# Prompt attention scores by three rounded products of high and low parts, and new sample value rows sent by GpSimd's queue, in a two-layer hybrid encoder step

## The chip, the cores and the metric

The kernel runs on one core of one Trainium2 chip. The metric is device time in microseconds of one execution. All times below are from runs and one profiled execution of the kernel before the change, with the TensorE clock granted in full (1.000) throughout.

## What is computed

The reference is one inference step of a two-layer encoder. 512 prompt frames and 8 x 16 sample frames, 640 columns in all, share the weights; the model width is 1024, the feed-forward width 2816. Per layer:

```
x += 1/2 * SwiGLU_1(RMSNorm(x))
z  = RMSNorm(x) @ w_in              # conv B | conv C | conv V | q | k | v | gates
conv branch: y_c = B * causal_depthwise_conv3(C * V)
attn branch: 8 heads x 64; prompt frames attend to the prompt up to their own 64-frame chunk,
             sample frames to 256 cached rows and their own 16
             s = (q @ k.T) * 64 ** -0.5 + rel_bias[distance];  softmax;  @ v
x += (sigmoid(g_c) * (y_c @ w_conv_out) + sigmoid(g_a) * (y_a @ w_attn_out)) @ w_o
x += 1/2 * SwiGLU_2(RMSNorm(x))
```

A final RMSNorm follows. The new keys, values and conv states are outputs too. Everything is float32.

## The kernel before

**Layout and arithmetic.** Features lie on the 128 partitions and the 640 columns (`T`) along the free dimension, in two halves of 320 (`HT`). Nearly all products with weights are computed from rounded parts: a float32 tile is split into a high part, which ScalarE rounds into an `fp32r` tile (`ACT.copy`), and a low part, which VectorE takes as the difference (`DVE.tensor_tensor`, subtract; `split`, `prep` and `flush`, L364 and L369). A product is then the sum of three TensorE matmuls, high x high, high x low and low x high (`multiply` L431, `block` L453; the matmul's line in the trace is L435 or L459). Weights come through SyncE's DMA queue in slabs (`raw`), are split into `whi` and `wlo` a slab or two ahead, and pairs of output tiles are formed by a scheme of seven products for eight (`seven`, L833), which runs as a generator: each `yield` lies behind six matmuls of 320 columns.

**The mixer of a layer.** `attention` (L1782) runs while the projections of `w_in` are computed. `qk(p)` (L1796) forms queries and keys of head pair p (two heads of 64 features, on partitions 0 to 63 and 64 to 127). In `both`, called by it, the last steps are: the second half of k (columns 320 to 639) is scaled behind the fifth product (`lo2`), q is completed behind the sixth (`up2`, then `queries`, which multiplies by `rr`, the reciprocal of the RMS, and by 64 ** -0.5, L1802), and the first half of k behind the seventh (`lo1`, L1368). `keys` sends k to the output by GpSimd's queue and copies the sample's columns.

**Prompt scores.** `scores(p)` (L1859) multiplies q by k for both heads of a pair, causal block rows i = 3, then 1, then 0 and 2, with (i + 1) * 128 key columns each. The two heads stand on the two halves of the partitions, so the contraction has 64 rows. Before the change q and k are plain float32 tiles, with two buffers each:

```
for i, c in spans:
    for e in range(2):
        r = slice(e * HD, (e + 1) * HD)
        PE.matmul(pss[e][:, c], qa[p][r, i * P : (i + 1) * P], ka[p][r, : (i + 1) * P],
                  start=True, stop=True)
```

The trace holds two records for each float32 matmul, so the 8 matmuls of one call of `scores` are 16 records (L1882). VectorE then adds the bias and takes the row maximum out of PSUM (L1888; `CUSTOM_DVE_ANT_0` in the trace, `ISA` in the instruction order), ScalarE does the softmax (L2082, L1899), TensorE transposes (L1919) and multiplies by v (L1951).

**What sets the order.** TensorE's order in this stage is the order of the code: calls of `scores`, `turn` and `values` with `fill(n)` between them, which runs n steps of the stream of projections (qk(1), qk(2), qk(3), then conv and gates). `scores(0)` comes two steps behind the end of qk(0); `scores(1)` and `scores(2)` three steps behind the end of their own qk; `scores(3)` three steps behind qk(3), and directly behind `values(1)`. The orders of VectorE, ScalarE, GpSimd and SyncE in this stage are made by the scheduler, by priorities (`soon` raises them).

**Samples.** For each of the 8 samples, `sscores` (L1986) loads cached keys into tiles of the tags "q" and "k" (the buffers that the prompt's q and k use) and cached values, clears a tile `vn` on GpSimd and copies the sample's 16 new value rows into it by a DMA from SyncE's queue (L2000). `svalues` (L2032) multiplies by them later (L2040).

Of the kernel before, what the change touches and what calls it, by code (L numbers as in the profile page):

```python
# [196 lines left out]
def trunk(ctx: ExitStack, tc: tile.TileContext, xin, wst, small, pbias, samplebias, kcache, vcache, gfin,  # L197
# [33 lines left out]
    def tmp(name):  # L231
        return tp.tile([P, UW], F32, tag="t", name=name)[:, :T]
# [191 lines left out]
    def soon():  # L424
        return tc.high_priority(offset=300)
# [908 lines left out]
    def mixer(l, after):  # L1334
        with tc.tile_pool(name=f"yp{l}", bufs=1, reuse_waits="tile") as yp, \
# [18 lines left out]
            with tc.tile_pool(name=f"mp{l}", bufs=2, reuse_waits="tile") as mp:  # L1354
# [3 lines left out]
                def pair(n, *given):  # L1358
                    return seven(f"{l}_{n}", pr, ops.X, *cs, *given)

                def upper(u):

                    return lambda pb: add(u[:, t1], pb, cs[0]), lambda pc: add(u[:, t2], pc, cs[1])

                def lower(g, scale=-1.0):

                    def by(c, src):
                        DVE.scalar_tensor_tensor(out=g[:, c], in0=src, scalar=scale, in1=rr[:, c],  # L1368
                                                 op0=ALU.mult, op1=ALU.mult)

                    def second(pa):
                        add(g[:, t2], pa, cs[2])
                        by(t2, g[:, t2])

                    return second, lambda pa: by(t1, pa)

                def both(n, u, g, third, last, scale=-1.0):

                    (up1, up2), (lo2, lo1) = upper(u), lower(g, scale)

                    def end1(pc):
                        up2(pc)
                        third()

                    def end2(pa):
                        lo1(pa)
                        last()

                    return pair(n, up1, lo2, end1, end2)

                def gate_pair(m):
                    u, g = gates[m], gates[m + 1] = tmp(f"g{l}_{m}"), tmp(f"g{l}_{m + 1}")
# [52 lines left out]
    class Operands:  # L1445
# [24 lines left out]
        def parts(self, hi, lo, z):  # L1470
            ACT.copy(hi, z)
            DVE.tensor_tensor(out=lo, in0=z, in1=hi.bitcast(F32), op=ALU.subtract)
# [309 lines left out]
    def attention(l, h, norms, stats, ops, mp, yas, ycp, both, others):  # L1782
# [12 lines left out]

        def qk(p):  # L1796

            q = qa[p] = mp.tile([P, T], F32, name=f"q{l}_{p}", tag="q")
            k = ka[p] = mp.tile([P, T], F32, name=f"k{l}_{p}", tag="k")

            def queries():
                DVE.scalar_tensor_tensor(out=q, in0=q, scalar=HD ** -0.5, in1=rr, op0=ALU.mult, op1=ALU.mult)  # L1802
                for e in range(2):
                    r = slice(e * HD, (e + 1) * HD)
                    POOL.tensor_copy(bd[r, :, p, e * TS : (e + 1) * TS],
                                     q[r, SEQ:].rearrange("p (b t) -> p b t", b=NB))

            def keys():
                POOL.dma_start(ko[l, :, p, :], k)
                POOL.tensor_copy(ks[:, p, :], k[:, SEQ:])  # L1810

            return both(f"qk{p}", q, k, queries, keys)

        def work():
            for p in range(1, npair):
# [43 lines left out]
        def scores(p):  # L1859

            heads = [2 * p + e for e in range(2)]
            bias, ss, st = [], [], []
            for hh in heads:
                n = f"{l}_{hh}"
                bias.append(mp.tile([P, SEQ], F32, name=f"bias{n}", tag="bias"))
                POOL.dma_start(bias[-1], pbias[l, hh])
                POOL.memset(bias[-1][0:CHUNK, SEQ - CHUNK :], NEG)

                ss.append(mp.tile([P, offs[-1] + SEQ], F32, name=f"s{n}", tag="s") if p % 2
                          else ycp[hh % 2].rearrange("p a t -> p (a t)"))  # L1870
                st.append(mp.tile([P, 2, NQ], F32, name=f"st{n}", tag="st", bufs=4))

            for rows in ((3,), (1,), (0, 2)):
                pss = [(pr if rows == (1,) else att)(f"pss{l}_{hh}_{rows[0]}") for hh in heads]
                spans, o = [], 0
                for i in rows:
                    spans.append((i, slice(o, o + (i + 1) * P)))
                    o = spans[-1][1].stop
                for i, c in spans:
                    for e in range(2):  # L1880
                        r = slice(e * HD, (e + 1) * HD)
                        PE.matmul(pss[e][:, c], qa[p][r, i * P : (i + 1) * P], ka[p][r, : (i + 1) * P],  # L1882
                                  start=True, stop=True)
                for i, c in spans:
                    for e in range(2):
                        w = (i + 1) * P
                        with soon():
                            DVE.tensor_tensor_reduce(  # L1888
                                out=ss[e][:, offs[i] : offs[i] + w], in0=pss[e][:, c],
                                in1=bias[e][:, SEQ - w :], scale=1.0, scalar=NEG, op0=ALU.add,  # L1890
                                op1=ALU.max, accum_out=st[e][:, 0, i : i + 1])
            for e, hh in enumerate(heads):
                weigh(hh, ss[e], st[e])
# [92 lines left out]
        def sscores(b):  # L1986
# [10 lines left out]

            vn = mp.tile([P, SEQ], F32, name=f"vn{n}", tag="bias")[:, :AW]
            POOL.memset(vn, 0.0)
            SP.dma_start(vn[:TS], vnew[rows])  # L2000
            for e, kc in enumerate(kcs):
                POOL.tensor_copy(kc[:, :, PAST:], ks[:, e * npair // 2 : (e + 1) * npair // 2, rows])
            pss = att(f"spss{n}")[:, :KS]
# [432 lines left out]
```

## Time and profile before

| | |
|---|---|
| median of 3 runs | 2481.9 us (2481.69 to 2482.22) |
| the profiled execution's own time | 2481.95 us |
| its span, first to last instruction | 2480.2 us |
| TensorE / VectorE / ScalarE / GpSimd busy | 99% / 88% / 56% / 13% of the span |
| prompt scores: 8 calls (4 head pairs, 2 layers) | 16 records each, 2.36 us each |
| the longest single wait of TensorE for another engine | 5.3 us, at the start of the program |

Busy time is the time in which an engine has an instruction under way. Matmuls overlap, and their recorded durations include the way through the array, so the pace of TensorE is read from the starts of successive matmuls, not from the mean duration of one. In the profile L followed by a number is the line in the kernel; PE is TensorE, PEld its weight loads, DVE VectorE, ACT ScalarE, POOL GpSimd, SP SyncE; a small q behind an engine's name is its queue. `pss` is the PSUM tile of the scores.

### The profile page before, as it was taken

Reading aid. Unit: us, or ns where it says so; the run is one execution under the profiler, and the core shown is the slowest. Engines: PE = TensorE matmul, PEld = TensorE weight load, DVE = VectorE, ACT = ScalarE, POOL = GpSimd, SP = SyncE. Lnnn points to the kernel's source line nnn. Section 1 sums busy time; section 2 is a strip of 40 time slices with the busy share of each in tenths; the row PEclk is TensorE's granted clock in tenths of the full one; section 3 lists DMA queues with packets and bytes.
Section 4 is the critical chain, followed back from the end, with each engine's and each line's share of the span. In section 5 each row is a group of like instructions: output and inputs, shape, how many; then the busy total and the mean of one; then the engine's idle time right before and its main releaser. Section 6 shows DMA issues by size and latency. Waiting matters only on the chain.

```text
span 2480.2 us, 44054 instructions
## 1 busy us (share of the span) xinstructions
PE 2467.0 (99%) x17264; PEld 2414.6 (97%) x17264; DVE 2182.4 (88%) x3643; ACT 1385.6 (56%) x2230; POOL 319.5 (13%) x483
## 2 busy tenths in 40 slices
PE   9999999999999999999999999999999999999999
PEld 8999999889999999999999999998899999999998
DVE  7999998888888899998799999988888889999997
ACT  6555556675555555555665555566655556555555
POOL 0111112211000001111001010121110000111111
PEclk9999999999999999999999999999999999999999
DMA  4443444335344334444334343452453333444444
GB/s 155 127 117 102 120 118 125 110 114 174 99 118 124 94 102 107 112 118 118 110 94 109 110 117 102 117 128 103 137 167 94 118 119 93 107 113 107 112 117 117
DMA packets 113520, 288.16 MB, mean 116 GB/s; under 512 B 12992, under 2 KB 52544, under 8 KB 113312
## 3 DMA queue, kind: packets, MB, share of 16 engines
q1 hardware_dynamic: 69552, 220.10, 27.0%
q0 software_dynamic: 43328, 64.99, 13.8%
q8 instruction: 135, 2.21, 0.4%
q14 instruction: 73, 0.60, 0.1%
q10 hardware_dynamic: 432, 0.25, 0.0%
HBM read 239.48 MB, written 7.94 MB: 100 GB/s over the span
## 4 chain that ended last, share of the span: by engine, by line
PE 93%; DVE 3%; ACT 2%; issue 1%; DMA 1%; SPq 0%; DVEq 0%; ACTq 0%; POOLq 0%
PE pab L459 12%; PE paa L459 11%; PE pcb L459 6%; PE daa L1144 6%; PE pca L459 5%; PE dab L1144 5%; PE po L435 5%; PE qa L459 4%; PE pbb L459 3%; PE dca L1144 3%; PE pba L459 3%; PE dcb L1144 2%; PE ma_cv L459 2%; PE ma_qk L459 2%; PE py L435 2%; PE pv L1835 2%
## 5 line engine op out<-in xcount | busy, mean ns | idle before, releaser
L364 ACT CAST whi<-raw 128x512 fp32r<-128x512 f32 (+1 forms) x577 | 501.7, 874 | 371.6 <-PE pbb L459 46.0
L369 DVE TENSOR_TENSOR wlo<-raw,whi 128x512 fp32r<-128x512 f32 (+1 forms) x577 | 577.1, 1002 | 137.1 <-ACT whi L364 132.9
L364 ACT CAST whi<-s 128x1024 fp32r<-128x1024 f32 (+1 forms) x162 | 152.8, 943 | 320.3 <-DVE s L296 113.9
L459 PE MATMUL pab<-xhib,whi 128*128 128x320 f32 x704 | 217.7, 309 | 0.0
L459 PE MATMUL pab<-xlob,whi 128*128 128x320 f32 x704 | 217.3, 309 | 0.0
L459 PE MATMUL pab<-xhib,wlo 128*128 128x320 f32 x704 | 217.3, 309 | 0.0
L459 PE MATMUL paa<-xhia,whi 128*128 128x320 f32 x640 | 197.8, 309 | 0.2 <-DVE ga L296 0.2
L459 PE MATMUL paa<-xhia,wlo 128*128 128x320 f32 x640 | 197.6, 309 | 0.0
L459 PE MATMUL paa<-xloa,whi 128*128 128x320 f32 x640 | 197.5, 309 | 0.0
L369 DVE TENSOR_TENSOR wlo<-s,whi 128x1024 fp32r<-128x1024 f32 (+1 forms) x162 | 176.4, 1089 | 4.4 <-ACT whi L364 4.4
L1166 POOL DMA_DIRECT2D x<-c_a x80 | 69.8, 1019 | 575.2 <-ACT ahia L1048 205.5
L1166 POOL DMA_DIRECT2D x<-c_b x72 | 63.1, 1011 | 583.2 <-ACT ahib L1048 205.4
L459 PEld LDWEIGHTS pab<-xhib,whi 128*128 128x128 f32 x704 | 132.1, 188 | 0.9 <-issue 0.9
L459 PEld LDWEIGHTS pab<-xlob,whi 128*128 128x128 f32 x704 | 132.1, 188 | 0.0
L459 PEld LDWEIGHTS pab<-xhib,wlo 128*128 128x128 f32 x704 | 132.1, 188 | 0.0
L459 PEld LDWEIGHTS paa<-xhia,whi 128*128 128x128 f32 x640 | 120.1, 188 | 1.1 <-DVE ga L296 0.5
L459 PEld LDWEIGHTS paa<-xloa,whi 128*128 128x128 f32 x640 | 120.1, 188 | 0.3 <-DVE xloa L703 0.3
L459 PEld LDWEIGHTS paa<-xhia,wlo 128*128 128x128 f32 x640 | 120.1, 188 | 0.2
L296 DVE TENSOR_TENSOR raw<-s,raw 128x512 f32<-128x512 f32 x162 | 110.8, 684 | 0.0
L459 PE MATMUL pcb<-xhib,wlo 128*128 128x320 f32 x352 | 108.9, 309 | 0.0
L459 PE MATMUL pcb<-xlob,whi 128*128 128x320 f32 x352 | 108.7, 309 | 0.0
L459 PE MATMUL pcb<-xhib,whi 128*128 128x320 f32 x352 | 108.7, 309 | 0.0
(909 smaller groups left out, 8200.5 us busy)
## 6 DMA issues: line engine op xcount, KB each, us to landing
raw<-in_wst SPq DMA_DIRECT2D x375, 512.0 KB, 3.6
x<-c_a POOLq DMA_DIRECT2D x80, 160.0 KB, 4.9
x<-c_b POOLq DMA_DIRECT2D x72, 160.0 KB, 4.2
lent<-in_wst POOLq DMA_DIRECT2D x36, 256.0 KB, 3.7
kc<-in_kcache SPq DMA_DIRECT2D x32, 256.0 KB, 4.9
vc<-in_vcache SPq DMA_DIRECT2D x16, 512.0 KB, 4.3
one<-in_wst POOLq DMA_DIRECT2D x32, 256.0 KB, 3.9
x<-u_a POOLq DMA_DIRECT2D x40, 160.0 KB, 4.1
```

What stands on the lines that cost most here:

```text
L296: DVE.tensor_tensor(out=out, in0=a, in1=b, op=op)
L364: ACT.copy(hi[:, d], src[:, c])
L369: DVE.tensor_tensor(out=lo, in0=src, in1=hi.bitcast(F32), op=ALU.subtract)
L435: PE.matmul(ps[:, a, :HT], w, x[a] if isinstance(x, tuple) else x[:, a * HT : (a + 1) * HT], start=first and j == 0 and not seeded, stop=l ...
L459: PE.matmul(ps, a, b, start=start and kp == 0 and j == 0, stop=stop and kp == NP - 1 and j == 2, skip_group_check=True)
L1144: PE.matmul(ps[u], w, y, start=start and i == 0 and j == 0, stop=i == 1 and j == 2, skip_group_check=True)
L1166: POOL.dma_start(x[ms[2 * u + r]][:, cols], z[:, u], accum_op=ALU.add)
L1835: PE.matmul(pv[t], xx[:, t * P : (t + 1) * P], w[:, kk * AW : (kk + 1) * AW], start=c == 0 and kk == 0 and j == 0, stop=c == KT // 2 - 1 a ...
```

## The change

1. `qk(p)` now puts q and k into temporary tiles (the pool of four that the gates and the conv use) and makes from each a pair of `fp32r` tiles of 512 columns, high and low. Each pair takes both buffers of its tag. `parts` does it: a rounding copy on ScalarE and a subtraction on VectorE. q is split in one piece of 512 columns after it is complete, k in two: columns 320 to 511 in the middle of `both` (the new argument `mid`), columns 0 to 319 behind its last product.
2. `scores(p)` computes each block as three matmuls into the same PSUM region: q high x k high, q low x k high, q high x k low, for both heads in turn, each on its 64 partitions. Its place in TensorE's stream is as it was.
3. The copy of a sample's new value rows into `vn` is issued from GpSimd's queue instead of SyncE's.

```diff
@@ -1374,9 +1374,14 @@
 
                     return second, lambda pa: by(t1, pa)
 
-                def both(n, u, g, third, last, scale=-1.0):
+                def both(n, u, g, third, last, scale=-1.0, mid=None):
 
                     (up1, up2), (lo2, lo1) = upper(u), lower(g, scale)
+
+                    def half(pa):
+                        lo2(pa)
+                        if mid:
+                            mid()
 
                     def end1(pc):
                         up2(pc)
@@ -1386,7 +1391,7 @@
                         lo1(pa)
                         last()
 
-                    return pair(n, up1, lo2, end1, end2)
+                    return pair(n, up1, half, end1, end2)
 
                 def gate_pair(m):
                     u, g = gates[m], gates[m + 1] = tmp(f"g{l}_{m}"), tmp(f"g{l}_{m + 1}")
@@ -1795,21 +1800,31 @@
 
         def qk(p):
 
-            q = qa[p] = mp.tile([P, T], F32, name=f"q{l}_{p}", tag="q")
-            k = ka[p] = mp.tile([P, T], F32, name=f"k{l}_{p}", tag="k")
+            q = tmp(f"q{l}_{p}")
+            k = tmp(f"k{l}_{p}")
+            qa[p], ka[p] = ([mp.tile([P, T], F32R, name=f"{z}{i}{l}_{p}", tag=z)[:, :SEQ]
+                             for i in ("hi", "lo")] for z in "qk")
+
+            def parts(zs, z, c):
+                hi, lo = (y[:, c] for y in zs)
+                with soon():
+                    ACT.copy(hi, z[:, c])
+                    DVE.tensor_tensor(out=lo, in0=z[:, c], in1=hi.bitcast(F32), op=ALU.subtract)
 
             def queries():
                 DVE.scalar_tensor_tensor(out=q, in0=q, scalar=HD ** -0.5, in1=rr, op0=ALU.mult, op1=ALU.mult)
+                parts(qa[p], q, slice(0, SEQ))
                 for e in range(2):
                     r = slice(e * HD, (e + 1) * HD)
                     POOL.tensor_copy(bd[r, :, p, e * TS : (e + 1) * TS],
                                      q[r, SEQ:].rearrange("p (b t) -> p b t", b=NB))
 
             def keys():
+                parts(ka[p], k, slice(0, HT))
                 POOL.dma_start(ko[l, :, p, :], k)
                 POOL.tensor_copy(ks[:, p, :], k[:, SEQ:])
 
-            return both(f"qk{p}", q, k, queries, keys)
+            return both(f"qk{p}", q, k, queries, keys, mid=lambda: parts(ka[p], k, slice(HT, SEQ)))
 
         def work():
             for p in range(1, npair):
@@ -1876,11 +1891,13 @@
                 for i in rows:
                     spans.append((i, slice(o, o + (i + 1) * P)))
                     o = spans[-1][1].stop
+                (qh, ql), (kh, kl) = qa[p], ka[p]
                 for i, c in spans:
-                    for e in range(2):
-                        r = slice(e * HD, (e + 1) * HD)
-                        PE.matmul(pss[e][:, c], qa[p][r, i * P : (i + 1) * P], ka[p][r, : (i + 1) * P],
-                                  start=True, stop=True)
+                    for j, (y, z) in enumerate(((qh, kh), (ql, kh), (qh, kl))):
+                        for e in range(2):
+                            r = slice(e * HD, (e + 1) * HD)
+                            PE.matmul(pss[e][:, c], y[r, i * P : (i + 1) * P], z[r, : (i + 1) * P],
+                                      start=j == 0, stop=j == 2)
                 for i, c in spans:
                     for e in range(2):
                         w = (i + 1) * P
@@ -1997,7 +2014,7 @@
 
             vn = mp.tile([P, SEQ], F32, name=f"vn{n}", tag="bias")[:, :AW]
             POOL.memset(vn, 0.0)
-            SP.dma_start(vn[:TS], vnew[rows])
+            POOL.dma_start(vn[:TS], vnew[rows])
             for e, kc in enumerate(kcs):
                 POOL.tensor_copy(kc[:, :, PAST:], ks[:, e * npair // 2 : (e + 1) * npair // 2, rows])
             pss = att(f"spss{n}")[:, :KS]
```

Where it moves instructions is seen in the orders. On TensorE, at the first block row of `scores(0)` in layer 0, before (`pss_0_3` is head 0's scores of block row 3, `k_0` and `q_0` the float32 keys and queries of head pair 0; behind `<-` the moving tile stands first, then the stationary one):

```order
L1882 MATMUL pss_0_3_5249<-k_0_5085,q_0_5084 128x512
L1882 MATMUL pss_1_3_5250<-k_0_5085,q_0_5084 128x512
L1882 MATMUL pss_0_1_5255<-k_0_5085,q_0_5084 128x256
L1882 MATMUL pss_1_1_5256<-k_0_5085,q_0_5084 128x256
L1882 MATMUL pss_0_0_5261<-k_0_5085,q_0_5084 128x128
L1882 MATMUL pss_1_0_5262<-k_0_5085,q_0_5084 128x128
```

and now (`khi`, `klo`, `qhi`, `qlo` are the parts):

```order
L1899 MATMUL pss_0_3_5263<-khi_0_5088,qhi_0_5086 128x512
L1899 MATMUL pss_1_3_5264<-khi_0_5088,qhi_0_5086 128x512
L1899 MATMUL pss_0_3_5263<-khi_0_5088,qlo_0_5087 128x512
L1899 MATMUL pss_1_3_5264<-khi_0_5088,qlo_0_5087 128x512
L1899 MATMUL pss_0_3_5263<-klo_0_5089,qhi_0_5086 128x512
L1899 MATMUL pss_1_3_5264<-klo_0_5089,qhi_0_5086 128x512
L1899 MATMUL pss_0_1_5273<-khi_0_5088,qhi_0_5086 128x256
L1899 MATMUL pss_1_1_5274<-khi_0_5088,qhi_0_5086 128x256
```

Each matmul became three in a row, with the two heads alternating as before: 24 matmuls for 8, and the low part of q is needed by the third of them, the low part of k by the fifth.

On VectorE, the rows ahead of the first reading of the scores (the `ISA` row, which waits for block row 3) at the same place, before (`mc_qk` and `ma_qk` are the projections in PSUM, `rrm` the reciprocal RMS, `s`, `raw` and `wlo` belong to the weights):

```order
L296 TENSOR_TENSOR q_0_5084<-mc_qk_5144,capsm_4817 128x320
L296 TENSOR_TENSOR raw_5194<-raw_5194 128x512
L1802 SCALAR_TENSOR_TENSOR q_0_5084<-q_0_5084,rrm_4818 128x640
L1368 SCALAR_TENSOR_TENSOR k_0_5085<-ma_qk_5091,rrm_4818 128x320
L369 TENSOR_TENSOR wlo_5201<-s_72_5196,whi_5200 128x512
L369 TENSOR_TENSOR wlo_5201<-raw_5194,whi_5200 128x512
L296 TENSOR_TENSOR raw_5158<-s_72_5196,raw_5158 128x512
L1888 ISA yc_0_4819,st_0_5244<-pss_0_3_5249,bias_0_5241 128x512
```

and now:

```order
L1812 TENSOR_TENSOR klo_0_5089<-k_0_5085,khi_0_5088 128x192
L296 TENSOR_TENSOR q_0_5084<-mc_qk_5148,capsm_4817 128x320
L296 TENSOR_TENSOR raw_5202<-raw_5202 128x512
L1815 SCALAR_TENSOR_TENSOR q_0_5084<-q_0_5084,rrm_4818 128x640
L1368 SCALAR_TENSOR_TENSOR k_0_5085<-ma_qk_5095,rrm_4818 128x320
L369 TENSOR_TENSOR wlo_5209<-s_72_5204,whi_5208 128x512
L1812 TENSOR_TENSOR qlo_0_5087<-q_0_5084,qhi_0_5086 128x512
L1812 TENSOR_TENSOR klo_0_5089<-k_0_5085,khi_0_5088 128x320
L369 TENSOR_TENSOR wlo_5209<-raw_5202,whi_5208 128x512
L1905 ISA yc_0_4819,st_0_5258<-pss_0_3_5263,bias_0_5255 128x512
```

Three subtractions came in: 192 columns of k ahead of q, 512 of q and 320 of k ahead of the second half of the weights' low part. The addition into `raw`, which the next weights need, now stands behind the readings of the scores.

On ScalarE, around the end of qk(0), up to the first copy out of PSUM that belongs to qk(1) (`c`, `capsm`: copies of projections; `whi`: weights), before:

```order
L364 CAST whi_5160<-raw_5158 128x1024
L863 COPY c_4829<-mc_qk_5144 128x320
L364 CAST whi_5200<-s_72_5196 128x512
L364 CAST whi_5200<-raw_5194 128x512
L851 COPY capsm_4817<-ma_qk_5228 128x320
```

and now:

```order
L364 CAST whi_5164<-raw_5162 128x1024
L863 COPY c_4829<-mc_qk_5148 128x320
L1811 CAST khi_0_5088<-k_0_5085 128x192
L364 CAST whi_5208<-s_72_5204 128x512
L364 CAST whi_5208<-raw_5202 128x512
L1811 CAST qhi_0_5086<-q_0_5084 128x512
L1811 CAST khi_0_5088<-k_0_5085 128x320
L851 COPY capsm_4817<-ma_qk_5242 128x320
```

Three rounding copies came in, and the two that the scores need last stand behind the roundings of two halves of weights.

## Prediction

> **What bounds the kernel now.** I read first the page's busy times and the chain that ended last.
>
> ```profile
> span 2480.2 us, 44054 instructions
> PE 2467.0 (99%) x17264; PEld 2414.6 (97%) x17264; DVE 2182.4 (88%) x3643; ACT 1385.6 (56%) x2230; POOL 319.5 (13%) x483
> PEclk9999999999999999999999999999999999999999
> PE 93%; DVE 3%; ACT 2%; issue 1%; DMA 1%; SPq 0%; DVEq 0%; ACTq 0%; POOLq 0%
> ```
>
> TensorE is busy for 99% of the span at its full clock and holds 93% of the chain: what its stream gains or loses comes out in the time, and work of another engine counts only where TensorE ends up waiting for it. The page does not say how fast TensorE goes. For that I take the chain in order of time, with the forms of two of its products behind it (`po` at line 435 has three matmuls of one form, one is shown).
>
> ```profile
> 428.53 13.62 PE pv L1835 x60
> 471.48 2.36 PE pss L1882 x16
> 487.29 2.36 PE pss L1882 x16
> 506.97 2.36 PE pss L1882 x16
> 526.38 2.36 PE pss L1882 x16
> 774.98 56.36 PE po L435 x384
> ...
> L1835 PE MATMUL pv<-whi,hhim x80: 389/389/504, 428.4 to 1684.8; 128*128 128x512 f32 x80
> L435 PE MATMUL po<-m_0hi,whi x32: 308/309/309, 774.8 to 2052.5; 128*128 128x320 f32 x32
> L1882 PE MATMUL pss<-k,q x128: 269/429/693, 471.4 to 1756.5; 64*128 64x512 f32 x32, 64*128 64x256 f32 x32, 64*128 64x128 f32 x32, 64*128 64x384 f32 x32
> ```
>
> Here one `fp32r` matmul of 512 columns takes 13.62 / 60 = 0.2270 us and one of 320 takes 56.36 / 384 = 0.1468, though each is recorded with 0.389 or 0.309: they overlap. The line through both is 0.418 ns a column and 13 ns a matmul. The prompt scores are on the chain four times in layer 0, with 2.36 us each; the last row shows 128 records in all, so 8 calls. That is what the change touches: 8 x 2.36 = 18.9 us, 0.8% of the span. Measurements of this kernel can tell about 0.2%, 5 us, from no change.
>
> **The scores themselves.** TensorE around the first call, from its timeline (start, duration):
>
> ```profile
> 471.17 0.31 PE L459 MATMUL ma_qk<-hhim,wlo 128*128 128x320 f32 x1
> 471.41 2.43 PE L1882 MATMUL pss<-k,q 64*128 64x512 f32 x16
> 473.77 0.41 PE L459 MATMUL mb_qk<-hhim,whi 128*128 128x320 f32 x1
> 474.02 0.31 PE L459 MATMUL mb_qk<-hlom,whi 128*128 128x320 f32 x1
> ```
>
> The step is 473.77 - 471.41 = 2.36 us. Around it 471.41 - 471.17 = 0.24 and 474.02 - 473.77 = 0.25 stand where the stream has 0.147: some 0.1 us more each at entry and exit, together 2.55. Each head has 128 + 256 + 384 + 512 = 1280 columns; at float32 they take 1280 x 4 x 0.418 ns = 2.14 us if the two heads go at the same time, and 4.28 one after the other. So they go at the same time, at a quarter of the rounded pace, and 2.55 - 2.14 = 0.41 is entry, exit and what a change of matmul costs.
>
> Now each head has three `fp32r` products: 3 x 1280 x 0.418 = 1.60 us, and 12 pairs by 13 ns, 0.16: 1.76 in place of 2.14, and the 0.41 stay (2.17 in all). That **saves 0.38 us a call**, if the heads still overlap; 0.50, if a pair costs 3 ns beside its columns in place of 13.
>
> The narrow pairs may be bound by their weights: a 128-column pair streams for 0.067 us, and its loads are not seen that fast anywhere. The excess at the exit, 0.25 - 0.147 = 0.10 us, is a load in the open. The nearest price is that: three 128-column pairs at 0.103 in place of 0.067 take back 3 x 0.036 = 0.11. Ends: nothing, or 0.11 with both heads' loads side by side. I take the 0.11: **0.27 saved a call, 8 x 0.27 = 2.2 us**. Loads of the two heads one after another are a rival below.
>
> A rule of the Trainium skill speaks against even this. Its page "TensorE: Matmul & The Clock Gate", section "Part 3: Packing small matmuls — row/col tiling", says that weight loads overlap matmuls in flight only when their row group differs. By that each of a head's products would wait for its own load; by the stream of 0.147 us above, in which every matmul uses all rows, it does not, so the sum keeps the overlap, and the rule is rival 2.
>
> **What feeds the scores.** Before, q and k were read as they were. Now each pair needs copies on ScalarE and subtractions on VectorE of 192, 512 and 320 columns. First VectorE and ScalarE ahead of `scores(0)`:
>
> ```profile
> 469.61 0.82 DVE L1802 SCALAR_TENSOR_TENSOR q<-q,rrm 128x640 f32<-128x640 f32 x1
> 470.35 0.48 DVE L1368 SCALAR_TENSOR_TENSOR k<-ma_qk,rrm 128x320 f32<-128x320 f32 x1
> 470.75 0.68 DVE L369 TENSOR_TENSOR wlo<-s,whi 128x512 fp32r<-128x512 f32 x1
> 471.35 0.78 DVE L369 TENSOR_TENSOR wlo<-raw,whi 128x512 fp32r<-128x512 f32 x1
> ...
> 468.81 0.62 ACT L364 CAST whi<-s 128x512 fp32r<-128x512 f32 x1 [3.04 <-DVE s L296]
> 469.73 0.63 ACT L364 CAST whi<-raw 128x512 fp32r<-128x512 f32 x1 [0.30 <-DVE raw L296]
> 471.57 0.43 ACT L851 COPY capsm<-ma_qk 128x320 f32<-128x320 f32 x1 [1.21 <-PE ma_qk L459]
> ```
>
> By the starts of VectorE's rows, 640 columns take 0.74 us, 320 take 0.40, 512 take 0.60, so 192 take 0.27. The first subtraction of k stands ahead of q: q's scaling then starts at 469.88, k's at 470.62, `wlo` at 471.02, q's low part at 471.62 (ready 472.3) and k's at 472.22 (ready 472.7). ScalarE sits idle for 1.21 us ahead of 471.57, so its order does not hold the copies up, the data do: q high from 470.70 to about 471.35, the last part of k high to 471.7. TensorE came at 471.41; it now starts the first pair near 471.76 (**0.35 lost**), is done with it 0.23 later, waits for q's low part until 472.3 (**0.3**), and for k's until 472.7 (**0.15**): 0.8 us. Queued behind the waiting matmuls is the whole projection stream, so this is paid in full.
>
> For `scores(1)` the same two engines, and their busy time in the stretch before it (columns: time, PE, PEld, DVE, ACT, POOL, clock, DMA share, GB/s):
>
> ```profile
> 485.22 0.49 DVE L1368 SCALAR_TENSOR_TENSOR k<-ma_qk,rrm 128x320 f32<-128x320 f32 x1
> 486.30 0.70 DVE L369 TENSOR_TENSOR wlo<-s,whi 128x512 fp32r<-128x512 f32 x1
> 485.88 0.20 ACT L2082 ACTIVATION_READ_ACCUMULATOR yc<-yc,st 128x1 f32 x1
> 487.22 0.70 PE L1882 MATMUL pss<-k,q 64*128 64x512 f32 x2
> 480.00:490.00 10.00, 10.00 (x69) 8.68 (x68) 8.85 (x17) 9.63 (x23) 2.10 (x6) 1.00 0.26 99
> ```
>
> In the new order q's low part stands directly behind this `wlo`, and q's high part behind this accumulator row, on a ScalarE that is full (9.63 of 10 us), so 0.27 from the 192 columns and what `scores(0)` gave late pass through: q low is ready near 488.25, k low near 488.65. TensorE comes 0.5 late (0.8 lost, 0.3 saved), at 487.7, has its first pair done at 487.95, waits 0.3, then 0.18: **about 0.5 us** (0 to 1.0).
>
> For the other two:
>
> ```profile
> 505.63 0.48 DVE L1368 SCALAR_TENSOR_TENSOR k<-ma_qk,rrm 128x320 f32<-128x320 f32 x1
> 522.89 0.48 DVE L1368 SCALAR_TENSOR_TENSOR k<-ma_qk,rrm 128x320 f32<-128x320 f32 x1
> ```
>
> k is complete at 506.1 for `scores(2)` at 506.97; k's and q's low parts cost 1.0 us behind it at once, so 0.1 (0 to 0.5). For `scores(3)` k is complete at 523.4 and TensorE comes at 526.38: nothing. **Stalls of a layer: 0.8 + 0.5 + 0.1 = 1.4, both layers 2.8 us** (bounds 0 and 4).
>
> **What else moves.** The three subtractions of a head pair take 0.27 + 0.60 + 0.40 us, so about 5 us of VectorE a layer, in a stage where it has some 1.2 us free in every 10. They push the weights' low parts back by a microsecond or so. Of TensorE's waits on weights the profile has next to none in 2480 us:
>
> ```profile
> PE poa L435 <- ACT whi L759: 5.3, 1, 5.3
> PE pca L459 <- DVE wlo L369: 0.5, 2, 0.3
> SPq L2000 <- POOL ss L2010: 56.9, 6, 10.4
> L2000 SPq DMA_DIRECT2D vn<-v x16: 512/513/947, 530.9 to 1841.9; - x16
> L1809 POOL DMA_DIRECT2D out_ko<-k x8: 539/544/544, 471.5 to 1752.3; - x8
> L2040 PE MATMUL spy<-vn,ss x128: 272/273/297, 574.2 to 1855.8; 128*32 128x128 f32 x128
> ```
>
> The longest on a low part is 0.3 us, and the weights are split a slab or two ahead; I cost the push at nothing (without that cover, up to 1 us a layer). The sixteen value copies leave SyncE, whose queue they held for 56.9 us in six waits with loads queued behind, and cost GpSimd 0.54 us each by its own row for k, 8.7 us, on an engine that is busy for 13%. First issued at 530.9, first read at 574.2: 43 us of room, so nothing on the path, in either direction. The cached keys, which share the tags of the parts, wait for the parts of head pair 2 to be read; their room is as large.
>
> **Sum.** The profiled execution took 2481.95 us (median 2481.9, no difference worth a correction): 2481.95 - 2.2 + 2.8 = 2482.55, for which I write **2482.5 us**: no change.
>
> **The rivals.**
>
> 1. *The waits cost nothing*: the parts are ready when TensorE comes. For it, ScalarE's idle 1.21 us; against it, VectorE's row of 471.35, behind which k's low part stands. Then 8 x 0.27 to 8 x 0.50 less: 2477.9 to 2479.8.
> 2. *The loads are the bound*: each pair is in the open with 0.103 us of loads, or the two heads' loads go one after another at 0.103 each. In the first case 12 x 0.103 = 1.24 join the 2.17, less one 0.10 that is in them: 3.31 against 2.55, 8 x 0.76 = 6.1, and stalls of about 1: 2489. In the second no pair is under 0.206, where 128, 256 and 384 columns stream for 0.067, 0.120 and 0.174: 3 x (0.139 + 0.086 + 0.032) = 0.77, so 2.94, 8 x 0.39 = 3.1 and stalls of 2.5: 2487.5. For it: nothing narrower than 320 columns in `fp32r` is in the trace. Against it, for loads of the float32 halves:
>
> ```profile
> 471.41 0.30 PEld L1882 LDWEIGHTS pss<-k,q 64*128 64x128 f32 x4 [0.19 <-issue]
> 471.41 0.70 PE L1882 MATMUL pss<-k,q 64*128 64x512 f32 x2
> ```
>
> Four loads start within 0.30 us while the first two matmuls run, so a head's next load does pass its running matmul.
> 3. *The heads no longer overlap* (the slower side): the two halves in `fp32r` go one after the other. The matmuls are then 24 x 13 ns + 6 x 1280 x 0.418 ns = 3.52 us a call, with the 0.41 3.93 against 2.55: 1.38 x 8 = 11.0. Low parts then come in time more often, so stalls of about 1 in all: 2494. The point from which it decides: an overlap that loses more than 0.6 us a call outweighs the margin of 5 us. Against it: the float32 halves overlap now, and nothing else in the order of the two heads changes.
> 4. *The edges go too*: if the 0.41 comes from the change between float32 and `fp32r`, it goes with it, 8 x 0.41 = 3.3: 2479.2, or below 2476.6 with rival 1.
>
> That the change does not do what it says has no room: the new order shows 24 matmuls for 8.
>
> **How the numbers follow.** Forecast with its own bounds (2480 to 2485) 0.62; rival 1 0.14; rival 4 0.08; rival 2 0.09; rival 3 0.07. The range takes the forecast and rivals 1 and 4: **2477.5 to 2486.5**. Faster by over 0.2% (below 2477) needs rivals 1 and 4 together: 0.04. Slower (above 2486.9) is rivals 2 and 3 but for a lighter form of rival 2, such as loads that go only partly one after another: 0.14. Within: 0.82.
>
> **What would show it.** The distance from the first row of `pss` to the next projection matmul, 2.36 now, is 2.0 to 2.1 us in `scores(3)`, which does not wait; 2.7 to 3.2 is rival 2, above 3.5 rival 3. Waits of TensorE on the parts of q and k, 0.8 us in `scores(0)` and 0.5 in `scores(1)`, on q low and k low above all. Pairs of rows that start together in TensorE's timeline. No new wait on `wlo` or `vn`. Wrong would be the sum if TensorE waited for weights in this stage, or if VectorE's delay reached the transposes and value products.

## The result, and the profile after

| | before | after |
|---|---|---|
| median of 9 runs | 2481.9 us (2481.48 to 2482.68) | 2488.96 us (2488.74 to 2489.86) |
| ratio to before, 95% interval | | 1.0028 (1.0019 to 1.0037) |
| span of the profiled execution | 2480.2 us | 2486.9 us |

The change costs 7.1 us; the prediction had no change, 2482.5, and a range that ended at 2486.5. The page of the kernel after:

```profile
span 2486.9 us, 44226 instructions
PE 2468.3 (99%) x17328; PEld 2417.2 (97%) x17328; DVE 2191.8 (88%) x3667; ACT 1394.4 (56%) x2254; POOL 323.3 (13%) x499
PE 88%; DVE 6%; ACT 3%; issue 2%; DMA 1%; SPq 0%; DVEq 0%; ACTq 0%; POOLq 0%
```

TensorE is busy for 1.3 us more in a span that is 6.7 us longer, so 5.4 us of the difference is time in which it stands idle. Its share of the chain fell from 93% to 88%, and VectorE, ScalarE and "issue" took the rest: the chain now runs through other engines for longer stretches, which says where to look and not how long TensorE waits. The list of its waits (us in total, times, longest; those at the start of the program left out):

```profile
PE ma_cv L459 <- ACT capsm L859: 1.8, 2, 0.9
PE pss L1899 <- DVE qlo L1812: 0.8, 4, 0.2
PE pss L1899 <- ACT khi L1811: 0.8, 2, 0.4
PE mc_qk L459 <- ACT c L863: 0.7, 2, 0.4
PE ma_qk L459 <- DVE k L296: 0.6, 2, 0.3
PE pca L459 <- DVE wlo L369: 0.5, 2, 0.3
PE ma_qk L459 <- ACT capsm L859: 0.3, 2, 0.2
```

The two rows of `pss` are the waits on parts that the prediction had. The rows with `capsm`, `c` and `k` are new and were not in it: TensorE wants to write a product of a projection into a PSUM tile (`ma_cv`, `mc_qk`, `ma_qk`) whose earlier content ScalarE or VectorE has not yet copied out. The `pca` row is as it was before.

Where the time is lost shows when the start of the same matmul is compared in both traces, through the stage. Each number is what TensorE fell behind (+) or gained there, in layer 0, worked out from these starts; layer 1 repeats every one within 0.03 us:

| place (time in the kernel before) | us |
|---|---|
| scores(0), to 473.8 | +0.83 |
| projections of qk(1), at 479.3 and 482.7 | +0.16, +0.49 |
| scores(1), to 489.6 | +0.45 |
| projections of qk(2), at 498.1 | +0.48 |
| scores(2), to 509.3 | -0.25 |
| projections of qk(3), at 513.8 | +0.44 |
| scores(3), to 528.7 | -0.24 |
| projections of the conv, at 533.2 | +1.17 |
| sum of a layer | +3.5 |

The scores make 0.8 of it and the projections 2.7, so 1.6 and 5.5 us in both layers. The two layers lose 7.0 us by these starts; the span grew by 6.7, since the kernel after had been 0.3 us ahead when it came to the stage, from the start of the program, where the runs differ by up to a microsecond. A wait of 0.90 in the list costs 1.17: its idle time is counted from the recorded end of the matmul before (0.31 behind its start), where the stream would have started the next one after 0.147, and the load of the first weights behind it lies open (0.25 against 0.147 between the starts of two matmuls).

A call of the scores that does not wait, scores(3) in the timeline after:

```profile
528.64 0.50 PE L1899 MATMUL pss<-khi,qhi 64*128 64x512 f32 x2
528.98 0.39 PE L1899 MATMUL pss<-khi,qlo 64*128 64x512 f32 x2
...
529.44 0.28 PE L1899 MATMUL pss<-khi,qhi 64*128 64x256 f32 x2
529.55 0.28 PE L1899 MATMUL pss<-khi,qlo 64*128 64x256 f32 x2
...
529.80 0.23 PE L1899 MATMUL pss<-khi,qhi 64*128 64x128 f32 x2
529.86 0.27 PE L1899 MATMUL pss<-khi,qlo 64*128 64x128 f32 x2
529.97 0.28 PE L1899 MATMUL pss<-klo,qhi 64*128 64x128 f32 x2
530.08 0.40 PE L1899 MATMUL pss<-khi,qhi 64*128 64x384 f32 x2
530.31 0.34 PE L1899 MATMUL pss<-khi,qlo 64*128 64x384 f32 x2
530.49 0.34 PE L1899 MATMUL pss<-klo,qhi 64*128 64x384 f32 x2
530.76 0.42 PE L459 MATMUL mb_cv<-hhim,whi 128*128 128x320 f32 x1
```

It takes 530.76 - 528.64 = 2.12 us (2.36 before). Each row is a pair (x2), one matmul of each head. The 2.12 us hold 12 pairs; one after the other the 24 matmuls would need 3.2 us by their columns alone (0.418 ns each), so the two heads go together. From one pair to the next there are 0.11 to 0.12 us at 256 columns, 0.06 and then twice 0.11 at 128, and 0.23 and then 0.18 at 384.

Why the copies come late is read from VectorE's and ScalarE's rows at two places, first behind scores(0). The kernel before, then the kernel after (rows picked out, start and duration; in brackets the idle time ahead and what ended it):

```profile
472.05 0.68 DVE L296 TENSOR_TENSOR raw<-s,raw 128x512 f32<-128x512 f32 x1
472.82 1.05 ACT L364 CAST whi<-raw 128x1024 fp32r<-128x1024 f32 x1 [0.82 <-DVE raw L296]
```

```profile
472.13 0.48 DVE L1812 TENSOR_TENSOR klo<-k,khi 128x320 fp32r<-128x320 f32 x1
472.53 0.68 DVE L369 TENSOR_TENSOR wlo<-raw,whi 128x512 fp32r<-128x512 f32 x1
473.30 0.69 DVE L1905 CUSTOM_DVE_ANT_0 yc<-pss,bias 128x512 f32<-128x512 f32 x1
475.22 0.69 DVE L296 TENSOR_TENSOR raw<-s,raw 128x512 f32<-128x512 f32 x1
475.99 1.05 ACT L364 CAST whi<-raw 128x1024 fp32r<-128x1024 f32 x1 [4.14 <-DVE raw L296]
```

In the slot ahead of the readings of the scores, where VectorE added the weights before, the subtractions stand now; the addition comes 3.2 us later, and ScalarE, idle for 4.14 us, rounds these weights at 475.99 instead of 472.82. What stands behind it on ScalarE, the softmax and in between the copies out of PSUM, moves with it. The second place is the conv, before and after:

```profile
526.38 1.23 DVE L369 TENSOR_TENSOR wlo<-raw,whi 128x1024 fp32r<-128x1024 f32 x1 [0.51 <-ACT whi L364]
527.57 0.69 DVE L1888 CUSTOM_DVE_ANT_0 s<-pss,bias 128x512 f32<-128x512 f32 x1
531.08 0.40 ACT L2082 ACTIVATE s<-s,st 128x128 f32<-128x128 f32 x1 [0.75 <-DVE st L2080]
532.57 0.40 ACT L859 COPY capsm<-ma_cv 128x320 f32<-128x320 f32 x1
533.17 0.31 PE L459 MATMUL ma_cv<-thi,whi 128*128 128x320 f32 x1
```

```profile
531.64 1.22 DVE L369 TENSOR_TENSOR wlo<-raw,whi 128x1024 fp32r<-128x1024 f32 x1
532.78 0.28 DVE L1905 CUSTOM_DVE_ANT_0 s<-pss,bias 128x128 f32<-128x128 f32 x1
534.36 0.40 ACT L2099 ACTIVATE s<-s,st 128x128 f32<-128x128 f32 x1 [1.95 <-DVE st L2097]
535.85 0.40 ACT L859 COPY capsm<-ma_cv 128x320 f32<-128x320 f32 x1
536.31 0.41 PE L459 MATMUL ma_cv<-thi,whi 128*128 128x320 f32 x1 [0.90 <-ACT capsm L859]
```

Before, the low part of a slab (1.2 us) was done ahead of the readings of scores(3). Now it stands in the midst of them, so the softmax starts at 534.36, 3.3 us later where TensorE itself is 2.1 us behind (528.67 became 530.76). The copy of `ma_cv` stands behind three softmax rows in ScalarE's order, and TensorE waits for it.

### The profile page after: what moved, and what is told of

It reads as the page before. It is cut to its first block, busy times and chain, and to the rows that moved or that the text cites. A ratio compares the mean times of both kernels' runs of the same rounds, so it can differ in the third digit from the quotient of the medians.

```text
span 2486.9 us, 44226 instructions
## 1 busy us (share of the span) xinstructions
PE 2468.3 (99%) x17328; PEld 2417.2 (97%) x17328; DVE 2191.8 (88%) x3667; ACT 1394.4 (56%) x2254; POOL 323.3 (13%) x499
## 4 chain that ended last, share of the span: by engine, by line
PE 88%; DVE 6%; ACT 3%; issue 2%; DMA 1%; SPq 0%; DVEq 0%; ACTq 0%; POOLq 0%
PE pab L459 12%; PE paa L459 11%; PE pcb L459 6%; PE daa L1144 6%; PE pca L459 5%; PE dab L1144 5%; PE po L435 5%; PE qa L459 4%; PE pbb L459 3%; PE dca L1144 3%; PE pba L459 3%; PE dcb L1144 2%; PE py L435 2%; PE pv L1850 2%; PE ma_cv L459 2%; PE qc L459 2%
## 5 line engine op out<-in xcount | busy, mean ns | idle before, releaser
L1166 POOL DMA_DIRECT2D x<-c_a x80 | 69.9, 1024 | 572.9 <-ACT ahia L1048 205.4
```

Source lines behind the costliest of these rows:

```text
L1166: POOL.dma_start(x[ms[2 * u + r]][:, cols], z[:, u], accum_op=ALU.add)
```

## The experiments

Theory A: VectorE's 5 us of subtractions a layer make ScalarE's and VectorE's copies out of PSUM late. Rivals: B, the narrow rounded matmuls themselves; C, the queue of the value rows; D, not VectorE's work but the places of the scores and of a few moved rows. All ratios are to the kernel before, run on the same chip; "lag" is what TensorE fell behind by the last matmul of the program in the profiled execution, from the starts of the same matmuls (up to 0.6 us of it arises outside this stage).

| run | median us | ratio, 95% interval | lag us |
|---|---|---|---|
| vn_only | 2482.03 | 0.9999 (0.9989 to 1.0009) | 0.2 |
| scores_only | 2489.49 | 1.0030 (1.0019 to 1.0041) | 7.6 |
| splits_fp32 | 2488.70 | 1.0026 (1.0016 to 1.0037) | 6.5 |
| hi_only | 2482.60 | 1.0001 (0.9992 to 1.0011) | -0.1 |
| q_sub_only | 2486.38 | 1.0017 (1.0007 to 1.0026) | |
| k_sub_only | 2489.50 | 1.0029 (1.0017 to 1.0041) | |
| late | 2487.82 | 1.0022 (1.0013 to 1.0031) | |
| s3_late | 2487.83 | 1.0023 (1.0013 to 1.0033) | |
| weights_first | 2502.39 | 1.0080 (1.0067 to 1.0093) | |
| weights_first_late | 2494.54 | 1.0052 (1.0039 to 1.0064) | |
| sub_pool | 2506.18 | 1.0095 (1.0079 to 1.0112) | |
| sub_pool_late | 2497.56 | 1.0063 (1.0048 to 1.0078) | |
| k_pool | 2496.58 | 1.0055 (1.0040 to 1.0070) | |
| far | 2494.79 | 1.0050 (1.0036 to 1.0064) | |
| pool_far | 2494.05 | 1.0048 (1.0035 to 1.0060) | |
| far_b | 2486.00 | 1.0015 (1.0005 to 1.0024) | 3.7 |
| pool_b | 2484.87 | 1.0010 (1.0000 to 1.0019) | 3.2 |
| pool_c | 2489.29 | 1.0028 (1.0018 to 1.0039) | 7.5 |

**The change in two halves.** `vn_only` is the kernel before with the third edit alone, `scores_only` the kernel after without it:

```
-            SP.dma_start(vn[:TS], vnew[rows])
+            POOL.dma_start(vn[:TS], vnew[rows])
```

> The kernel before with only the value rows sent by GpSimd's queue. If the queue has a part in the 7.0 us: some microseconds slower than 2481.9 us. If all of it is in the scores and their parts: 2481.9, within 0.5.

> The changed kernel with the value rows back on SyncE's queue. If the scores and parts hold all of the loss: 2489, with the waits of TensorE as in the changed kernel (capsm, c and k, 3.4 us; parts, 1.6 us). If the queue has a part: less than 2488.

2482.03 and 2489.49: the queue has no part in it that these runs can see, and C falls.

**The splits without the rounded products, the products without the subtractions.** `splits_fp32` makes all parts and multiplies the float32 q and k; `hi_only` leaves the subtractions out (edits against the kernel after):

```
-                    for j, (y, z) in enumerate(((qh, kh), (ql, kh), (qh, kl))):
+                    for j, (y, z) in enumerate(((qf[p], kf[p]),)):
```

```
-                    DVE.tensor_tensor(out=lo, in0=z[:, c], in1=hi.bitcast(F32), op=ALU.subtract)
...
+                    for j, (y, z) in enumerate(((qh, kh), (qh, kh), (qh, kh))):
```

> The changed kernel, parts of q and k made as there, but the scores multiplied from the float32 q and k (one matmul a block and head): the parts are written and never read. Theory A, the copies and subtractions delay VectorE and ScalarE, so that copies out of the projections' PSUM come late and TensorE waits for them: the waits on capsm, c and k stay (about 1.1 to 1.4 us a layer beside 0.25 of restart each, 2.7 us a layer in all), those on the parts go, and a call of the scores is 2.36 us again: 2486 to 2488. Rival B, the narrow rounded products cost the time: 2482.

> The changed kernel without the subtractions: the three products of a block are all of high parts, so the scores are not those of the reference. TensorE has the same 24 matmuls a call and ScalarE the same copies, VectorE 5 us a layer less. Theory A with VectorE as the engine that delays: the waits on capsm, c and k go for the most part, as do those on low parts; 8 x 0.25 us are saved and the wait for k high (0.35 a layer) stays: 2480 to 2482. If ScalarE's copies delay as much: 2484 or more. Rival B (narrow products): 2486 or more.

TensorE's waits in `splits_fp32`, then in `hi_only` (here and below the first rows, but for those at the start of the program):

```profile
PE ma_cv L459 <- ACT capsm L859: 1.8, 2, 1.0
PE ma_qk L459 <- DVE wlo L369: 1.4, 4, 0.4
PE pca L459 <- DVE wlo L369: 0.5, 2, 0.3
```

```profile
PE pss L1898 <- ACT khi L1811: 0.7, 2, 0.4
PE pca L459 <- DVE wlo L369: 0.5, 2, 0.3
```

With the float32 matmuls of before, and parts that nobody reads, 6.5 us are lost, somewhat more than expected. The wait on `capsm` at the conv is there. Those on `c` and `k`, which were expected to stay, are not; in their place TensorE waits for weights' low parts, 1.4 us, the very wait that the prediction had put at nothing. With all 24 matmuls and all of ScalarE's copies, but no subtraction, no wait on `capsm`, `c` or `k` is left, and the time is that of before. B falls. In `hi_only` the calls of scores(1) and scores(3) gain 0.24 and 0.26 us, as in the kernel after. ScalarE's copies are nearly free, and not quite: scores(2) waits 0.35 us for k's high part, so the four calls gain 0.5 us a layer in place of 1.0, and the projections still fall behind by 0.35 us a layer (2.7 in the kernel after). So the run ends at 2482.6 and not at the 2480 to 2482 that were expected.

**Half of the subtractions.** `q_sub_only` and `k_sub_only` subtract only one of the two, the other low part being replaced by a high part:

```
+                    if zs is qa[p]:
+                        DVE.tensor_tensor(out=lo, in0=z[:, c], in1=hi.bitcast(F32), op=ALU.subtract)
```

> The changed kernel without k's subtractions; the third product takes k's high part again, so the scores are not those of the reference. VectorE has 2.4 us a layer added in place of 5. If the loss grows with VectorE's work: PSUM waits of about 1.3 us a layer (2.7 with all, 0 with none), and with the waits on q's parts 2485 to 2486. If it hangs on the moved row alone (the weights' addition stands ahead of the readings of scores(0) again in this kernel): no PSUM waits in the first half of the stage, 2483.5.

> The changed kernel without q's subtraction; the second product takes q's high part again, so the scores are not those of the reference. VectorE has 2.7 us a layer added. As q_sub_only: 2485 to 2486 if the loss grows with VectorE's work, 2483.5 if it hangs on the moved row.

Waits in `q_sub_only`, then in `k_sub_only` (the first rows):

```profile
PE ma_qk L459 <- ACT capsm L859: 1.2, 2, 0.6
PE pss L1900 <- ACT ya L1972: 0.9, 2, 0.5
PE ma_cv L459 <- ACT capsm L859: 0.7, 2, 0.4
```

```profile
PE pss L1900 <- ACT khi L1811: 2.2, 4, 0.7
PE pss L1900 <- DVE klo L1813: 1.8, 4, 0.6
PE pss L1900 <- ACT ya L1972: 1.0, 2, 0.5
PE ma_cv L459 <- ACT capsm L859: 0.7, 2, 0.4
```

With q's half the loss is 4.3 us, somewhat over half. The weights' addition stands ahead of the readings of scores(0) in this kernel, and up to 498 only 0.13 us a layer is lost at projections where the kernel after loses 1.1. In `k_sub_only` the addition stands ahead too, at 472.89, and under 0.1 us is lost there; in `splits_fp32` it comes behind the readings, at 476.97, and 1.1 us is lost. So that part goes with the moved row, though the runs with the addition ahead also have less to subtract. The waits of the second half of the stage stay in `q_sub_only`. With k's half the loss is as large as with both, 7.4 us, of which 4.0 are waits on k's parts. So the loss is not proportional to VectorE's work: each of these orders pays it at other places.

**Other places for the scores and the moved rows.** `late` moves scores(0) and scores(1) one step back, `s3_late` scores(3) two, `weights_first` raises the weights' rows in the priorities, `weights_first_late` does all three:

```
-        fill(2)
+        fill(3)
         scores(0)
...
-        fill(4)
+        fill(3)
         turn(0, 0)
```

```
+                    fill(2)
                     scores(p + 2)
```

```
-            with tc.high_priority(offset=150):
+            with tc.high_priority(offset=300):
```

> The changed kernel with scores(0) and scores(1) one step (six matmuls of 320, 0.88 us) later in TensorE's stream. If the waits on the parts are a cost of their own: both calls lose them, about 0.9 and 0.6 us a layer, 3 us in all, so 2486. If they only take in advance what TensorE would wait for the late PSUM copies anyway: some of it comes back at the waits on capsm, c and k, and the time is 2487.5 to 2489.

> The changed kernel with scores(3) two steps later in TensorE's stream (behind the first products of the conv). The wait on capsm behind scores(3), 1.1 us a layer, is where ScalarE's copy of the conv's first product stands behind softmax rows that wait for VectorE's reading of scores(3). If that reading's place makes the wait: it moves or goes, and up to 2.2 us are saved (2487). If VectorE is late whatever stands there: the same 2489, with the wait elsewhere.

> The changed kernel with the weights' additions and low parts raised in the scheduler's priorities (150 to 300), so that on VectorE the addition that the next weights wait for stands ahead of the readings of scores(0) again, as before the change. If that one moved row is what holds ScalarE back (it idled 4.1 us for it): the waits of TensorE at 479 and 482 (0.6 us a layer) go, and perhaps those that follow; the low parts come 0.6 to 1.2 us later, so scores(0) and scores(1) wait more: 2486 to 2490. If VectorE is simply too full: waits on capsm, c and k of 2.5 us a layer as now.

> The same, with scores(0) and scores(1) one step later and scores(3) two steps later. If moved rows and the places of the scores make the loss: 2483 to 2485.5. If VectorE is too full: 2486 or more.

By their medians `late` and `s3_late` lose 1.1 us less than the kernel after, which their intervals hardly tell from it. In `late` the scores gained what was expected only in part, and the waits on `c` grew from 0.7 to 1.1: some of it came back at the next copies. The trace of `s3_late` is clearer than its median: the wait on `capsm` at the conv, 1.8 us in the kernel after, is gone from TensorE's list, and by the starts scores(3) and the conv together lose 0.1 us a layer, where they lose 0.9 in the kernel after. The subtractions are the same in both, so at the conv the place of scores(3) and its readings decides, as D has it; without the subtractions the old place costs only 0.2 us there (`hi_only`), so it takes both. `weights_first` was a miss, by 12 us on the wrong side: the priorities moved the weights' low parts ahead of k's last scaling too, and the scores waited 10.1 us for k's high part. `weights_first_late` keeps 7.3 us of that wait. Neither separates the theories.

**The subtractions on GpSimd, and room for them.** `sub_pool` subtracts on GpSimd, `k_pool` only k's; `sub_pool_late` has the step of `late`. `far` and `pool_far` move scores(0) and scores(1) by five steps and scores(2) and scores(3) by two, with VectorE and with GpSimd; `far_b` and `pool_b` move the first transposes and value products four steps back as well; `pool_c` moves scores(0), scores(1), scores(3) and the first transposes and value products a step less.

```
-                    DVE.tensor_tensor(out=lo, in0=z[:, c], in1=hi.bitcast(F32), op=ALU.subtract)
+                    POOL.tensor_tensor(out=lo, in0=z[:, c], in1=hi.bitcast(F32), op=ALU.subtract)
```

> The changed kernel with the three subtractions of a head pair on GpSimd in place of VectorE. Theory A (VectorE's added work makes the PSUM copies late): the waits on capsm, c and k go, 2.7 us a layer, whatever happens to the parts. If GpSimd is as fast as VectorE the parts come as before: 2483 to 2484; if it is two or three times slower, scores(0) and scores(1) wait 1 to 2 us more each: 2487 to 2490. Rival: the order on ScalarE alone makes the copies late, and the waits on capsm, c and k stay.

> Both edits: subtractions on GpSimd, scores(0) and scores(1) one step later. Theory A: no wait on PSUM copies and less wait on the parts, so below sub_pool by 1 to 3 us, and at best 8 x 0.25 below the kernel before: 2480 to 2485. Rival as for sub_pool: above 2485.

> The changed kernel, at its own places, with k's two subtractions on GpSimd and q's on VectorE: VectorE has 2.4 us a layer added in place of 5. Theory A: about half of the 2.7 us a layer of PSUM waits go; k's low part comes from GpSimd 0.5 to 1 us later than from VectorE, so scores(0) and scores(1) wait that much more: 2486 to 2490.

In `sub_pool` the waits on `capsm`, `c` and `k` are gone, but TensorE, held up by the parts, leaves its neighbours more time, so this shows less than `hi_only` does. A subtraction of 512 columns takes GpSimd 1.7 us:

```profile
PE pss L1899 <- POOL qlo L1812: 9.4, 6, 1.9
PE pss L1899 <- POOL klo L1812: 2.8, 7, 0.8
L1812 POOL TENSOR_TENSOR qlo<-q,qhi x8: 1619/1688/1707, 472.4 to 1775.7; 128x512 fp32r<-128x512 f32 x8
```

The losses of 24 us here, 15 in `sub_pool_late` and 14 in `k_pool` were all larger than expected. The price of one subtraction is within the two to three times that was assumed (VectorE takes 0.77 us for these 512 columns); what was left out is GpSimd's order and the clock. For scores(0) q's low part starts on GpSimd at 472.42, behind the copies of the sample's columns and the sending of k (471.43 on VectorE in the kernel after), and k's follows it, to 474.92. And waits of this length lowered the granted clock, as the last section shows.

> The changed kernel (subtractions on VectorE) with scores(0) and scores(1) five steps later and scores(2) and scores(3) two steps later, the transposes and value products where they were. No scores wait for parts, so 1.8 us a layer come back at once (2485); the waits on PSUM copies stay if VectorE is too full in the stage, and change place if they hang on where the readings fall: 2481 to 2486.

> The subtractions on GpSimd and the scores in the places of the run before. Theory A: VectorE has no added work, so no waits on PSUM copies, and GpSimd's slow parts (1.7 us for 512 columns) come in time: each of the 8 calls costs 0.25 us less than in the kernel before: 2480 to 2481. Rival (the parts' cost only moves): 2483 or more.

> Scores as in far (five and two steps later) with the transposes and value products of head pair 0 four steps later too; subtractions on VectorE. If VectorE's work makes the PSUM copies late: no wait on parts, but 1 us or more a layer on capsm, c, k or yc: 2482 to 2486. If only order and places made them: 2480 to 2481.

> The same places, subtractions on GpSimd. If VectorE's work makes the PSUM copies late: none of these waits, 0.25 us less a call, 2480 to 2481, and below far_b. If the engine does not matter: as far_b.

> As pool_b with scores(0) and scores(1) four steps later in place of five, scores(3) one in place of two. GpSimd's parts come just in time or up to 0.5 us late: within 1 us of pool_b.

`far` and `pool_far` missed for a plain reason: the transposes of head pair 0 had stayed, and waited 5.3 and 5.7 us for the softmax; the lowered clock behind these waits took another 5 and 3 us by the estimate of the last section. With the transposes moved, no call waits for parts in `far_b` and `pool_b`, and the same order of TensorE gives 2486.0 with VectorE and 2484.87 with GpSimd, both above before (the interval of `pool_b` just reaches 1.0000; all its executions lie above all those of the kernel before). Waits in `far_b`, then in `pool_b` (that on `pca`, as before, left out):

```profile
PE ma_cv L459 <- DVE yc L296: 1.0, 2, 0.5
PE ma_qk L459 <- ACT capsm L851: 0.5, 2, 0.3
PE ma_qk L459 <- DVE k L296: 0.4, 2, 0.2
```

```profile
PE ma_qk L459 <- ACT capsm L851: 2.8, 2, 1.4
```

`pool_c` lost the room again (2489.3, not within 1 us of `pool_b`). So A does not hold in its simple form: with VectorE free of the subtractions `pool_b` still waits 1.4 us a layer for a copy, at one place. There ScalarE rounds 1024 columns of weights at 507.89 and copies `ma_qk` behind it, at 508.84; in `far_b` the copy stands ahead of the rounding, at 507.77, and TensorE waits for it 0.3 us at most. Taking the work off VectorE was enough in `hi_only`, where the rest stayed where it was; in `pool_b` it was not.

## Why the prediction was wrong, step by step

- **What bounds the kernel**: right. TensorE's stream sets the time, and each loss is a wait of it.
- **The products**: right in mechanism and size. The heads overlap and a call that does not wait gains 0.24 to 0.25 us (0.27 predicted). Rivals 2 and 3 are out: a call takes 2.12 us, not 2.7 or more. By the rule of the Trainium skill that the prediction weighed ("TensorE: Matmul & The Clock Gate", section "Part 3: Packing small matmuls — row/col tiling"), each pair would wait for its load; the trace disagrees, with 0.18 between the second and the third pair of 384 columns, which stream for 0.174.
- **The waits on parts**: scores(0) and scores(1) had 0.8 and 0.5 us predicted, against a gain of 0.27 each; the measured +0.83 and +0.45, with a gain of 0.25, make them 1.08 and 0.70. They stand where the prediction put them, on k's high part and q's and k's low parts. scores(2) had 0.1 and waits for nothing. In both layers the scores cost 1.6 us where the sum had 0.6. This alone would have been within the range.
- **The step that failed: "I cost the push at nothing (without that cover, up to 1 us a layer)".** It measured 2.7 us a layer, 5.5 in all. The prediction asked what the push does to the weights' low parts, which have room in the kernel after (no new wait on `wlo` in its list), and took the absence of waits in the profile of before for room everywhere. It did not follow the copies out of PSUM, which have little: in the kernel before the copy of `ma_cv` ended at 532.97, and TensorE wrote that tile again at 533.17, 0.2 us later. Nor did it follow the row that the instruction orders of the change had shown to move, the addition behind the readings of scores(0): ScalarE's next row waits for it, and the softmax and the copies stand behind that. Its signs of being wrong, a wait for weights or a delay of the transposes and value products, do not name the copies either.
- **The queue of the value rows and the cached keys**: right. `vn_only` shows no cost and no gain of the queue, and TensorE's list of waits in the kernel after has no row for `vn` or the cached keys.
- That VectorE's subtractions are the cause is shown at the places of the change: without them the loss is gone, and with them and the products of before it is 6.5 us. That it passes through the order, a moved row or the place of the readings, is shown for the conv (`s3_late`, `hi_only`); for the first half of the stage it is borne out by four runs (`q_sub_only`, `k_sub_only`, `hi_only` and `splits_fp32`), none of which moves that row alone. Open is why k's half alone loses as much as both, and whether some order of the stage would leave the 8 x 0.25 = 2 us of gain; none of those tried did, and none beat the kernel before.

## What to carry to other kernels

When an engine in a full stage gets more work, list every PSUM tile that the bounding engine writes again there, and read how long ahead the copy that frees it ends; a list of waits without such a wait does not show that margin. Then follow the rows that the new order moves to the engine that needs them next, and to everything behind that in its order. A saving of 2 us in the stream was not worth 5 us of work a layer on the engine that feeds it, even though that engine was busy for only 88%.

## What the runs showed of the hardware

Matmuls of 64 rows in two halves run in pairs in `fp32r` as in float32. At 256 columns a pair costs its columns and little more (0.11 to 0.12 us, 0.107 by 0.418 ns a column). At 128 columns, where the columns take 0.054, the second and third pair cost 0.11 us too, about the 0.10 of a load in the open; only the first, behind a pair of 256, takes 0.06.

A wait has a second price when it is long. In `weights_first`, TensorE stood for 2.25 us (its row, then the two stretches behind it; the granted clock is the column after the five engines):

```profile
473.92 0.50 PE L1899 MATMUL pss<-khi,qhi 64*128 64x512 f32 x2 [2.25 <-ACT khi L1811]
...
474.00:476.50 2.50, 2.50 (x25) 1.79 (x25) 1.75 (x3) 2.33 (x2) 0.32 (x1) 0.81 0.36 138
476.50:479.00 2.50, 2.50 (x11) 2.50 (x10) 2.50 (x13) 0.00 (x0) 0.00 (x0) 0.50 0.61 197
```

The clock granted was 0.81 on the mean from 474 to 476.5 and 0.50 from there to 479. At 0.50, with 1.00 before it, the low clock began at about 475.6 by this mean, some 1.6 us after work had begun again. The Trainium skill, "TensorE: Matmul & The Clock Gate", section "Part 1: The HAM clock gate (the "warmup" mystery)", puts the return to the slow clock at an idle window of about 3.4 us; here 2.25 us were enough. Such stretches at 0.50 add up to 17 us in `sub_pool`, 14 in `weights_first`, 10 in `far` and 7 in `pool_far`. At half the pace each costs half its length, by estimate 8.5, 7, 5 and 3 us of the losses of these runs, beside the waits themselves. In the kernel after, with waits of 0.9 us at most, the clock is 1.00 in every stretch of this stage.
